# Trunk kernel: the two heads of a pair take turns in stick-breaking attention, and the sums for the seven products are spaced wider, their second parts on Pool

## The chip, the cores and the metric

One Trainium2 chip, one core. The metric is the device time of one launch in microseconds (us). A core has five engines that run beside each other, each through its own instructions in order: TensorE (PE, matmuls and transposes), VectorE (DVE), ScalarE (ACT), GpSimd (POOL) and SyncE (SP, which issues the DMAs). They wait for each other through semaphores.

## The reference

A decoder trunk of two layers on 1024 tokens of width 1024, all in float32. Cut to what matters:

```python
for l in range(DEPTH):                                   # 2
    h = rmsnorm(x, norm1[l])
    proj = h @ w_in[l]
    qa, ka, va, qb, kb, vb, gate_pre = jnp.split(proj, splits, axis=-1)
    o_a = dilated_mixture(qa, ka, va)                    # 3 groups of 4 heads of 64
    o_b = stick_breaking_attention(qb, kb, vb)           # 4 heads of 64
    gates = sigmoid(gate_pre + b_gate[l])
    x = x + (g_a * (o_a @ w_br[l, :256]) + g_b * (o_b @ w_br[l, 256:])) @ w_o[l]
    h2 = rmsnorm(x, norm2[l])
    a, v = split(h2 @ w_up[l])
    x = x + (gelu(causal_conv(a)) * v) @ w_down[l]
return rmsnorm(x, norm_f)

# stick_breaking_attention, one head:
z = q @ k.T * scale
log_stay = where(key < query, log_sigmoid(-z), 0)
later = reverse_cumsum(log_stay) - log_stay
o = where(key < query, exp(log_sigmoid(z) + later), 0) @ v
```

## The kernel before

**Numbers in two parts.** A float32 product is done as three matmuls: each operand is split into a first part `hi` (a ScalarE copy, line 123) and a second part `lo = src - hi` (a VectorE subtraction, line 124). `split` does both; it is used for weights (`w_hi`, `w_lo`), for transposed probabilities (`sbh`, `sbl` in the stick stage, `p0h`, `p0l` in the near stage) and for the sums below (`t_hi`, `t_lo`).

**Two streams on TensorE.** In the mixer of a layer, `attend` walks a list of attention items, and between an item's small steps it draws steps of the dense products from `Dense` (`dense.advance(rate)`; the rate for stick items is 0.68 of a dense step per small step). A dense step is six matmuls of a projection. The order of TensorE's instructions is the order in which they are written out. On the other engines the order is made by a planner when the program is built: it takes instructions in order of rank as they become ready by its own times, and what stands in `tc.high_priority(offset=AHEAD)` ranks 200 places earlier.

**Stick items.** There are sixteen in a layer: two pairs `pr`, two heads `s` of a pair, four blocks `qp` of 256 queries. `stick_item(pr, s, qp)` gives two score steps and qp + 1 pairs of a `turn` and an `apply`. A score step (`score(a)`, a block of 128 queries against L = 128 (2 qp + a + 1) keys) makes `z` on TensorE, masks its last 128 columns on VectorE (line 610), takes two sigmoids on ScalarE (`beta`, line 611, and `stay`, line 612), and then on VectorE a running product of `stay` from the right (the scan, line 614) and `beta * stay` (line 615). `turn` transposes blocks of `beta` on TensorE (line 625) and splits them; `apply` multiplies them with the values (line 636), and the last one of an item adds the halves up (`fold`). The score steps of the *next* item are written in between the steps of the present one. In the kernel before, one head of a pair goes through qp = 0, 1, 2, 3, and then the other.

After the sixteen stick items come four near items (`N00` to `N11`: scores `z`, `p`, the exponential of `p`, transposes `t`, products `o` on line 700) and sixteen far items.

**Sums of h.** Later dense units are computed in blocks, with seven products in place of eight. Their right-hand sides are sums of quarters of `h`, made once in a layer by `block_sums` in four series of four pieces (128 x 512 each). Series 3 and 1 need three Pool operations a piece (lines 871 to 873, `h_sum`); series 2 and 4 go on from them with two VectorE operations a piece (lines 882 and 883). Then each piece is split by `in_two`. The list that `series` makes has one entry for each call of `dense.aside()`, which goes with every `dense.advance`: piece i begins at entry i * gap and is split `lag` entries later. Series 3 may begin once item `B17`, the last stick item, is done, and series 1 once `N01`'s scores are. The first unit that uses the sums (`pair_v`, seven products, tiles `i_a`, `i_c`) comes after `N11`'s scores; its first Pool operation is line 936, `u`.

Of the kernel before, what the change touches and what calls it, by code (L numbers as in the profile page):

```python
# [11 lines left out]
ALU = mybir.AluOpType  # L12
# [28 lines left out]
RATE = (0.68, 0.85, 0.72, 0.62)  # L41
# [5 lines left out]
def f32(ap):  # L47
    return ap.bitcast(F32)
# [3 lines left out]
def trunk_kernel(ctx, tc, x, norm1, w_in, b_gate, w_br, w_o, norm2, w_up, conv_w, conv_b, w_down, norm_f, out, depth=None, probe=None):  # L52
    nc = tc.nc
    act, dve, pe, pool = nc.scalar, nc.vector, nc.tensor, nc.gpsimd
# [55 lines left out]
    def bank(tag, name):  # L110
        return ps.tile([P, 512], F32, tag=tag, name=name)
# [4 lines left out]
    def big(name, dtype=F32):  # L116
        return sb.tile([P, 2, T], dtype, tag="e8", bufs=6, name=name)

    def quarter(name, dtype=F32, c=HF):
        return sb.tile([P, 2048 // c, c], dtype, tag="xa", bufs=4, name=name)  # L120

    def split(hi, lo, src):
        act.copy(hi, src)  # L123
        dve.tensor_tensor(lo, src, f32(hi), ALU.subtract)  # L124
# [292 lines left out]
    S, B = {}, {}  # L417
# [152 lines left out]
    def scores(o, qt, ql, k):  # L570
        pe.matmul(o, qt, k, start=True, stop=False, skip_group_check=True)
        pe.matmul(o, ql, k, start=False, stop=True, skip_group_check=True)
# [17 lines left out]
    def stick_item(pr, s, qp):  # L590
        if "ob" not in R:
            R["ob"] = big("ob")
        q, k, vt, ob = R["qb", pr], R["kb", pr], R["vb"], R["ob"]
        hd = 2 * pr + s
        rows, st, shared = {}, {}, {}

        def score(a):
            i = 2 * qp + a
            L = P * (i + 1)
            bt = rows[a] = sb.tile([P, T], F32, tag="p4", bufs=4, name="beta")  # L600
            if a == 0:
                st[0] = big("stay")
            sv = st[0][:, a, :]
            for c0 in range(0, L, 512):
                w = min(512, L - c0)
                z = bank("s", "z")
                scores(z[:, :w], *(t[:, s, i * P : i * P + P] for t in q), k[:, s, c0 : c0 + w])
                with tc.high_priority(offset=AHEAD):
                    if c0 + w == L:
                        dve.tensor_tensor(z[:, w - P : w], z[:, w - P : w], mask_b, ALU.add)  # L610
                    act.activation(bt[:, c0 : c0 + w], z[:, :w], AF.Sigmoid)
                    act.activation(sv[:, c0 : c0 + w], z[:, :w], AF.Sigmoid, scale=-1.0)  # L612
            rev = sv[:, 0:L][:, ::-1]
            dve.tensor_tensor_scan(rev, rev, zero[:, 0:1].to_broadcast([P, L]), 1.0, ALU.mult, ALU.add)  # L614
            dve.tensor_tensor(bt[:, 0 : L - 1], bt[:, 0 : L - 1], sv[:, 1:L], ALU.mult)

        def blocks(kb):

            return [(j, a) for j in range(2) for a in range(2) if kb + j <= 2 * qp + a]

        def turn(kb):
            tp = bank("t", "sb_t")
            todo = blocks(kb)
            for c, (j, a) in enumerate(todo):
                pe.transpose(tp[:, c * P : c * P + P], rows[a][:, (kb + j) * P : (kb + j + 1) * P], ident)
            shared[kb] = parts(tp, len(todo) * P, "sb")

        def apply(kb):
            last = kb == 2 * qp
            if kb == 0:  # L630
                shared["o"] = bank("o", "sb_o")[:, :256]
            o = shared["o"]
            for j in range(2):
                c = P if last and j else 0
                for p in (0, 1):
                    pe.matmul(
                        o[:, c:256],
                        vt[(kb + j) // 4][:, (kb + j) % 4, hd, :],
                        shared[kb][p][:, 256 * j : 256 * j + 256 - c],
                        start=(kb == 0 and j == 0 and p == 0),  # L640
                        stop=(last and j == 1 and p == 1),
                        skip_group_check=True,
                    )
            if last:
                fold(ob[64 * s : 64 * s + 64, pr, qp * 256 : (qp + 1) * 256], o)
                if (pr, s, qp) == (1, 1, 3):
                    nc.sync.dma_start(obd, ob)

        sc = [lambda: score(0), lambda: score(1)]
        return sc, [(lambda kb=kb: turn(kb), lambda kb=kb: apply(kb)) for kb in range(0, 2 * qp + 2, 2)]  # L650
# [209 lines left out]
    def block_sums():  # L860


        keep = {}

        def first(t, a, b, i):
            if i == 0:
                if "r" not in keep:
                    keep["r"] = quarter("h_sum")
                new_s(t)
            r, (ah, al), (bh, bl) = keep["r"][:, i, :], a()[i], b()[i]  # L870
            pool.tensor_tensor(r, f32(al), f32(bl), ALU.subtract)
            pool.tensor_tensor(r, r, f32(ah), ALU.add)
            pool.tensor_tensor(r, r, f32(bh), ALU.subtract)

        def further(t, a, i):
            if t == 4:

                S[4] = half(0, 0)
            elif i == 0:
                new_s(t)  # L880
            r, (ah, al) = keep["r"][:, i, :], a()[i]
            dve.tensor_tensor(r, f32(ah), r, ALU.subtract)
            dve.tensor_tensor(r, r, f32(al), ALU.add)

        def in_two(t, i):
            split(*S[t][i], keep["r"][:, i, :])

        b11, b12, b21, b22 = (lambda n=n, k=k: half(n, k) for k in range(2) for n in (1, 0))
        todo = []

        def series(after, t, f, lag, gap):

            at = {}
            for i in range(4):
                at.setdefault(i * gap, []).append(lambda i=i: f(i))
                at.setdefault(i * gap + lag, []).append(lambda i=i: in_two(t, i))
            for k in range(3 * gap + lag + 1):
                todo.append((after, lambda fs=at.get(k, ()): [g() for g in fs]))

        series({"B17"}, 3, lambda i: first(3, b22, b12, i), 4, 3)  # L900
        series({"N01s"}, 1, lambda i: first(1, b12, b11, i), 4, 3)
        series({"N11s"}, 2, lambda i: further(2, b22, i), 1, 1)
        series({"plain"}, 4, lambda i: further(4, b21, i), 1, 1)
        return todo
# [180 lines left out]
    def mixer(l, pending):  # L1085
# [31 lines left out]
        items = []  # L1117
        for pr in range(2):
            for i in range(8):
                needs = ["b1"] if pr else []  # L1120
                items.append((f"B{pr}{i}", needs, [], RATE[0], lambda pr=pr, i=i: stick_item(pr, i // 4, i % 4)))
        for pr in range(2):
            for s in range(2):
                items.append((f"N{pr}{s}", [f"0{pr}"], ["v0"], RATE[1], lambda pr=pr, s=s: near_item(pr, s)))
# [590 lines left out]
    def first():  # L1715
        gb = sb.tile([P, T], F32, tag="ot", name="gb")
        warm = sb.tile([P, 8], F32, tag="ss", bufs=2, name="warm")
        act.activation(warm[:, 0:1], eps, AF.Sqrt)
        wp = bank("t", "warm")
        for _ in range(WARM):  # L1720
            pe.matmul(wp[:, 0:P], ident, ident, start=True, stop=True)
        for n in range(2):
            new_h(n)
            for c in range(4):
                t0 = n * HF + c * P
                xr = sb.tile([P, T], F32, tag="p4", bufs=4, name="xr")
                nc.sync.dma_start(xr, xin[t0 : t0 + P, :])
                if n == 0 and c == 0:
                    nc.sync.dma_start(gb, norm1[0].partition_broadcast(P))
                sq = sb.tile([P, T], F32, tag="ql", bufs=2, name="xsq")  # L1730
                ss = sb.tile([P, 8], F32, tag="ss", bufs=2, name="ss")
                act.activation(sq, xr, AF.Square, accum_out=ss[:, 0:1])
                act.activation(ss[:, 1:2], ss[:, 0:1], AF.Sqrt, bias=eps[:, 0:1], scale=1.0 / D)
                dve.reciprocal(ss[:, 2:3], ss[:, 1:2])
                for e0 in (0, 4):
                    hd = slice(e0 * P, (e0 + 4) * P)
                    dve.scalar_tensor_tensor(xr[:, hd], xr[:, hd], ss[:, 2:3], gb[:, hd], ALU.mult, ALU.mult)
                    tp = bank("s", "x_t")
                    for e in range(4):
                        pe.transpose(tp[:, e * P : (e + 1) * P], xr[:, (e0 + e) * P : (e0 + e + 1) * P], ident)  # L1740
                    tv = tp.rearrange("p (e t) -> p e t", e=4)
                    hi, lo = (h[:, e0 : e0 + 4, c * P : (c + 1) * P] for h in H[n])
                    split(hi, lo, tv)
                yield
# [46 lines left out]
```

## Time and profile before

| | |
|---|---|
| median of 3 runs | 2751.21 us (2749.49 to 2751.34) |
| the profiled execution | 2748.3 us, of it 2746.1 us from the first to the last instruction |
| granted TensorE clock, mean | 0.992 |
| busy: TensorE / VectorE / ScalarE / Pool | 2669.7 / 1989.7 / 1351.9 / 687.1 us |
| stick items, layer 0 / layer 1 | about 70 to 244 us / 1429 to 1605 us |
| near items, layer 0 / layer 1 | to about 330 us / 1690 us |

In the profile's rows the engine that is busy for nearly all of a stretch is the one that bounds it, and a row of the waits names, for an engine's pause, the instruction that waited and the one that it waited for, then the total in us, how often, and the longest. Window rows give a stretch, its length, and then the busy time of each engine in it; groups of instructions give the count, the busy time and the mean of one in ns; a tile's rows give shortest, median and longest in ns. The granted clock is a share of full speed.

### The profile page before, as it was taken

To read this page: it belongs to the slowest core of one execution; us is meant where nothing else is said; L and a number is where in the kernel's file an instruction comes from. 1 tells how busy PE (TensorE), PEld (TensorE's weight loads), DVE (VectorE), ACT (ScalarE), POOL (GpSimd) and SP (SyncE) were. 2 spreads that over 40 slices of the span, in tenths; PEclk is the share of its full clock that TensorE was granted. 3 is DMA by queue.
4 is the path that set the end of the run, shared out by engine and by line. 5 is a ranking of instruction groups with operands and counts; after the bars stand their busy time and mean duration, and the time that the engine had idled before them with its cause. 6 is when DMAs were issued, how large, how long until landed. Compare 5 with 4: busy or idle time off the path is not lost.

```text
span 2746.1 us, 36499 instructions
## 1 busy us (share of the span) xinstructions
PE 2669.7 (97%) x13066; PEld 2235.0 (81%) x13066; DVE 1989.7 (72%) x2952; ACT 1351.9 (49%) x2494; POOL 687.1 (25%) x485
## 2 busy tenths in 40 slices
PE   8999999989999999999999999999799999999999
PEld 8878888868878888878888788888688788887888
DVE  5877656555779888887657775565658788988865
ACT  5655545465445555422335555455535455554225
POOL 1005011222134433331120051112312443443200
PEclk9999999999999999999999999999899999999999
DMA  5012268664334444688401122785732444446963
GB/s 151 27 44 81 63 188 247 212 205 134 89 115 162 146 154 139 223 319 299 170 31 35 44 81 88 201 252 189 235 94 77 142 141 158 166 141 238 346 235 123
DMA packets 362305, 424.77 MB, mean 155 GB/s; under 512 B 25244, under 2 KB 289804, under 8 KB 360588
## 3 DMA queue, kind: packets, MB, share of 16 engines
q1 hardware_dynamic: 362124, 422.44, 46.9%
q8 instruction: 103, 1.69, 0.3%
q14 instruction: 78, 0.64, 0.1%
HBM read 282.78 MB, written 139.59 MB: 154 GB/s over the span
## 4 chain that ended last, share of the span: by engine, by line
PE 47%; DVE 5%; DMA 1%; issue 1%; ACT 1%; POOL 1%; DVEq 0%; SPq 0%; ACTq 0%; POOLq 0%
PE d_ps L1539 4%; PE d_ps L1541 4%; PE d_ps L1540 4%; PE u_a L854 3%; PE u_a L856 3%; PE u_a L855 3%; PE u_c L856 1%; PE u_c L854 1%; PE u_c L855 1%; PE i_a L854 1%; PE i_a L855 1%; PE i_a L856 1%; PE o_ps L149 1%; PE o_ps L151 1%; PE o_ps L150 1%
## 5 line engine op out<-in xcount | busy, mean ns | idle before, releaser
L123 ACT CAST w_hi<-up_a 128x512 fp32r<-128x512 f32 x240 | 149.5, 623 | 193.9 <-PE u_a L855 42.2
L124 DVE TENSOR_TENSOR w_lo<-up_a,w_hi 128x512 fp32r<-128x512 f32 x240 | 223.6, 938 | 20.4 <-ACT w_hi L123 20.4
L1547 DVE TENSOR_TENSOR x<-x,d_ps 128x512 f32<-128x512 f32 (+1 forms) x228 | 152.3, 672 | 78.0 <-PE d_ps L1541 77.3
L1285 POOL TENSOR_TENSOR cv<-cv 128x512 f32<-128x512 f32 x88 | 132.6, 1518 | 276.8 <-DVE g L124 144.7
L124 DVE TENSOR_TENSOR g<-cv,g 128x512 fp32r<-128x512 f32 x154 | 167.6, 1089 | 8.7 <-ACT g L123 6.2
L124 DVE TENSOR_TENSOR w_lo<-w_raw,w_hi 128x512 fp32r<-128x512 f32 x152 | 116.7, 773 | 66.9 <-ACT w_hi L123 63.4
L123 ACT CAST w_hi<-w_raw 128x512 fp32r<-128x512 f32 x152 | 93.9, 620 | 120.0 <-PE o_ps L150 64.4
L124 DVE TENSOR_TENSOR w_lo<-in_a,w_hi 128x512 fp32r<-128x512 f32 x120 | 90.9, 757 | 85.2 <-ACT w_hi L123 85.0
L123 ACT CAST w_hi<-in_a 128x512 fp32r<-128x512 f32 x120 | 74.5, 621 | 133.0 <-PE i_c L855 52.3
L1539 PE MATMUL d_ps<-gd_in,w_hi 128*128 128x512 f32 (+1 forms) x340 | 130.7, 384 | 6.1 <-ACT g L123 5.8
L1541 PE MATMUL d_ps<-gd_in,w_lo 128*128 128x512 f32 (+1 forms) x340 | 130.5, 384 | 0.0
L1540 PE MATMUL d_ps<-gd_in,w_hi 128*128 128x512 f32 (+1 forms) x340 | 130.3, 383 | 0.0
L856 PE MATMUL u_a<-hh,w_lo 128*128 128x512 f32 x320 | 124.7, 390 | 4.2 <-DVE w_lo L124 4.2
L854 PE MATMUL u_a<-t_hi,w_hi 128*128 128x512 f32 x320 | 124.7, 390 | 0.7 <-ACT u L1420 0.7
L854 PE MATMUL u_a<-hh,w_hi 128*128 128x512 f32 x320 | 124.6, 390 | 0.6 <-DVE u L1437 0.6
L856 PE MATMUL u_a<-t_hi,w_lo 128*128 128x512 f32 x320 | 124.5, 389 | 0.0
L855 PE MATMUL u_a<-hl,w_hi 128*128 128x512 f32 x320 | 124.5, 389 | 0.0
L855 PE MATMUL u_a<-t_lo,w_hi 128*128 128x512 f32 x320 | 124.5, 389 | 0.0
L614 DVE TENSOR_TENSOR_SCAN stay<-stay,zero 128x128 f32<-128x128 f32 (+3 forms) x64 | 86.8, 1357 | 38.7 <-ACT stay L612 38.6
L1539 PE MATMUL d_ps<-gd_in,wd 128*128 128x512 f32 (+1 forms) x292 | 113.9, 390 | 0.0
L1541 PE MATMUL d_ps<-gd_in,wd 128*128 128x512 f32 (+1 forms) x292 | 112.8, 386 | 0.0
L1540 PE MATMUL d_ps<-gd_in,wd 128*128 128x512 f32 (+1 forms) x292 | 112.8, 386 | 0.0
(397 smaller groups left out, 8593.7 us busy)
## 6 DMA issues: line engine op xcount, KB each, us to landing
gd<-g SPq DMA_DIRECT2D x154, 512.0 KB, 3.3
gd_in<-gd SPq DMA_DIRECT2D x154, 512.0 KB, 6.2
up_a<-in_w_up_dram SPq DMA_DIRECT2D x80, 512.0 KB, 5.4
t_kq<-tk SPq DMA_DIRECT2D x32, 768.0 KB, 6.3
wd_raw<-in_w_down_dram SPq DMA_DIRECT2D x22, 1024.0 KB, 9.5
w_raw<-in_w_in_dram SPq DMA_DIRECT2D x80, 256.0 KB, 3.3
in_a<-in_w_in_dram SPq DMA_DIRECT2D x40, 512.0 KB, 5.8
gin<-gs SPq DMA_DIRECT2D x32, 512.0 KB, 4.4
```

Source lines behind the costliest of these rows:

```text
L123: act.copy(hi, src)
L124: dve.tensor_tensor(lo, src, f32(hi), ALU.subtract)
L149: pe.matmul(o, lh, rh, start=(first and i == 0), stop=False, skip_group_check=share)
L614: dve.tensor_tensor_scan(rev, rev, zero[:, 0:1].to_broadcast([P, L]), 1.0, ALU.mult, ALU.add)
L854: pe.matmul(o, w[0][:, c], rh, start=(first and i == 0), stop=False, skip_group_check=True)
L855: pe.matmul(o, w[0][:, c], rl, start=False, stop=False, skip_group_check=True)
L856: pe.matmul(o, w[1][:, c], rh, start=False, stop=(last and i == 3), skip_group_check=True)
L1285: return lambda: pool.tensor_tensor(dst, a, b, ALU.subtract)
L1539: pe.matmul(o[:, sub], wh[:, c], gh[:, sub], start=(i == 0 and k in (0, 4, 5)), stop=False, skip_group_check=True)
L1540: pe.matmul(o[:, sub], wh[:, c], gl[:, sub], start=False, stop=False, skip_group_check=True)
L1541: pe.matmul(o[:, sub], wl[:, c], gh[:, sub], start=False, stop=(i == m - 1), skip_group_check=True)
L1547: dve.tensor_tensor(x, x, o[:, sub], ALU.add)
```

## The change

The two heads of a pair take turns: the items of a pair now run as (s, qp) = (0,0), (1,0), (0,1), (1,1), (0,2), (1,2), (0,3), (1,3). In `block_sums`, the pieces of series 3 and 1 begin five entries apart instead of three, and their second parts are subtracted on Pool instead of VectorE; the ScalarE copy is the same, and so are series 2 and 4.

```diff
         def in_two(t, i):
-            split(*S[t][i], keep["r"][:, i, :])
+            if t in (1, 3):
+                hi, lo = S[t][i]
+                act.copy(hi, keep["r"][:, i, :])
+                pool.tensor_tensor(lo, keep["r"][:, i, :], f32(hi), ALU.subtract)
+            else:
+                split(*S[t][i], keep["r"][:, i, :])
...
-        series({"B17"}, 3, lambda i: first(3, b22, b12, i), 4, 3)
-        series({"N01s"}, 1, lambda i: first(1, b12, b11, i), 4, 3)
+        series({"B17"}, 3, lambda i: first(3, b22, b12, i), 4, 5)
+        series({"N01s"}, 1, lambda i: first(1, b12, b11, i), 4, 5)
         series({"N11s"}, 2, lambda i: further(2, b22, i), 1, 1)
         series({"plain"}, 4, lambda i: further(4, b21, i), 1, 1)
...
         for pr in range(2):
             for i in range(8):
                 needs = ["b1"] if pr else []
-                items.append((f"B{pr}{i}", needs, [], RATE[0], lambda pr=pr, i=i: stick_item(pr, i // 4, i % 4)))
+                items.append((f"B{pr}{i}", needs, [], RATE[0], lambda pr=pr, i=i: stick_item(pr, i % 2, i // 2)))
```

## The prediction

> **What bounds the kernel now.** The page comes first, then the waits of TensorE, since only what ends one of its pauses can move the end.
>
> ```profile
> span 2746.1 us, 36499 instructions
> PE 2669.7 (97%) x13066; PEld 2235.0 (81%) x13066; DVE 1989.7 (72%) x2952; ACT 1351.9 (49%) x2494; POOL 687.1 (25%) x485
> PE sb_t L625 <- DVE beta L615: 12.5, 10, 2.4
> PE o L700 <- DVE p0l L124: 4.5, 2, 2.2
> PE o L700 <- ACT p0h L123: 0.5, 2, 0.3
> PE z L571 <- ACT stay L612: 1.2, 1, 1.2
> ```
>
> TensorE is busy 97% of the span and the change gives it the same matmuls, so all that can be won is its idle time, 2746.1 - 2669.7 = 76 us, and slow clock behind a pause. The last four lines (total, times, longest) are the only pauses in the two stretches that the diff touches: stick-breaking transposes waiting for VectorE's `beta`, and near-attention products waiting for `p0l`. Together 18.7 us, over two layers.
>
> Where do the first fall? The window view, cut at the first transpose of an item (layer 0: the last item of pair 0, then pair 1), gives per row the length and the busy time of PE, PEld, DVE, ACT, POOL, then the granted clock.
>
> ```profile
> 138.62:154.12 15.50, 14.04 (x79) 11.77 (x78) 10.16 (x20) 6.83 (x16) 0.00 (x0) 1.00 0.24 75
> 154.12:160.19 6.07, 6.07 (x32) 5.10 (x31) 4.47 (x7) 3.24 (x7) 0.00 (x0) 1.00 0.24 70
> 160.19:169.09 8.90, 8.90 (x49) 7.41 (x47) 7.54 (x11) 5.97 (x14) 0.00 (x0) 1.00 0.01 2
> 169.09:181.23 12.14, 10.86 (x61) 9.03 (x59) 9.89 (x14) 7.26 (x15) 0.00 (x0) 1.00 0.15 44
> 181.23:199.22 17.99, 15.55 (x79) 13.06 (x79) 11.94 (x21) 9.38 (x20) 0.00 (x0) 0.91 0.10 30
> 199.22:205.30 6.08, 6.08 (x32) 5.09 (x31) 4.53 (x8) 3.59 (x9) 0.00 (x0) 1.00 0.11 43
> 205.30:214.04 8.74, 8.74 (x48) 7.45 (x47) 7.65 (x11) 5.58 (x13) 0.00 (x0) 1.00 0.29 90
> 214.04:225.29 11.25, 11.14 (x62) 9.35 (x61) 8.75 (x11) 6.85 (x14) 1.90 (x2) 1.00 0.07 25
> ```
>
> The rows show one head climbing through its four query blocks (qp 0 to 3: about 6, 9, 11 and 15 us), and then the other. Length minus PE time is the pause at the start of a row: 1.46 at 138.62 (qp 3), 0, 0, 1.28 at 169.09 (qp 2), 2.44 at 181.23 (qp 3), 0, 0, 0.11. So it is the larger blocks that wait, at the top of a climb. Each row holds the scores of the *next* item beside the transposes of its own; VectorE is busy 74, 85 and 91% of PE's time over rows two to four, so its queue fills as the head climbs and empties in the long row.
>
> The clock costs more on top:
>
> ```profile
> 184.00:187.20 3.20, 3.20 (x9) 2.66 (x10) 2.43 (x5) 1.09 (x4) 0.00 (x0) 0.50 0.00 0
> 265.70:269.10 3.40, 3.40 (x10) 2.71 (x11) 1.57 (x3) 0.00 (x0) 3.40 (x4) 0.50 0.28 82
> 269.20:272.60 3.40, 3.40 (x21) 2.87 (x20) 1.37 (x2) 3.34 (x6) 3.14 (x3) 1.00 0.00 0
> 1543.60:1549.00 5.40, 4.64 (x17) 3.93 (x18) 4.53 (x9) 1.93 (x5) 0.00 (x0) 0.70 0.04 10
> 1605.00:1648.00 43.00, 40.51 (x216) 33.78 (x215) 35.24 (x58) 25.39 (x56) 27.71 (x21) 1.00 0.29 88
> ```
>
> After the pause of 2.44 us the clock is 0.50 for about 3.4 us; the same after layer 0's `p0l` pause (third row: 21 matmuls in the next 3.40 us against 10), and 0.70 on average behind layer 1's long stick pause. Half of 3.4 us is lost each time, 1.7. Layer 1's `p0l` pause costs no clock (last row, 1.00), nor does the 1.46 above. The Trainium skill, "TensorE: Matmul & The Clock Gate", Part 1, says that the array falls to half clock after an idle window of about 3.4 us; the pauses here are shorter and three of four lost it, so the trace decides. By that page no clock would come back and the sum below would be 5.1 us smaller.
>
> **Part 1: heads take turns.** An item does exactly what it did; only the order in a pair changes, from 0,1,2,3,0,1,2,3 to 0,0,1,1,2,2,3,3. The last item of a pair stays the last, so the sum of dense steps drawn before it, the units that wait for its scores and the store of `ob` keep their place to within two steps; the zero fill that waits for the third item comes some four steps earlier, on Pool, idle there. These cost nothing.
>
> What moves is VectorE's load per row. For the step into the qp 3 block the prices are:
>
> ```profile
> L614 DVE TENSOR_TENSOR_SCAN stay<-stay,zero 128x1024 f32<-128x1024 f32 x4 | 9.2, 2292 | 4.6 <-ACT stay L612 4.6
> L614 DVE TENSOR_TENSOR_SCAN stay<-stay,zero 128x896 f32<-128x896 f32 x4 | 8.1, 2025 | 3.4 <-ACT stay L612 3.4
> L614 DVE TENSOR_TENSOR_SCAN stay<-stay,zero 128x768 f32<-128x768 f32 x4 | 7.0, 1757 | 3.0 <-ACT stay L612 3.0
> L614 DVE TENSOR_TENSOR_SCAN stay<-stay,zero 128x640 f32<-128x640 f32 x4 | 6.0, 1492 | 1.3 <-ACT stay L612 1.3
> L615 DVE TENSOR_TENSOR beta<-beta,stay 128x1023 f32<-128x1023 f32 x4 | 4.9, 1217 | 0.0
> L615 DVE TENSOR_TENSOR beta<-beta,stay 128x895 f32<-128x895 f32 x4 | 4.3, 1084 | 0.1
> L615 DVE TENSOR_TENSOR beta<-beta,stay 128x767 f32<-128x767 f32 x4 | 3.8, 948 | 0.0
> L615 DVE TENSOR_TENSOR beta<-beta,stay 128x639 f32<-128x639 f32 x4 | 3.3, 820 | 0.1
> ```
>
> Scans and products of a qp 3 block are 2.29 + 2.03 + 1.22 + 1.08 = 6.6 us, of a qp 2 block 1.76 + 1.49 + 0.95 + 0.82 = 5.0. Before, every qp 2 row (10.9 us of PE) carries the 6.6; now one of two carries 5.0 and the other comes after that lighter row. A qp 3 row (14 us) carries 6.6 once, where it carried a small block before: 3 us of work more, but in the row with most room (10.16 of 14.04 busy). The equal steps are the new thing, and each is easier than the climb that it replaces: the same row, a shorter chain to the transposes. Into qp 0 and 1 the rows at 160.19 and 205.30 start without a pause even as climbs.
>
> So the climbs fall from twelve to six in a layer, and each stands behind a level step. Bounds for the 12.5 us: nothing saved (if the queue just fills elsewhere), or all of it. Half by count is 6.3 left; I take 5 left, since the worst (169.09, then 181.23) are two climbs in a row with a backlog handed on, which the new order doesn't have. Saved: 7.5, and both clock losses behind the 2.4 us pauses, 3.4. The 1.2 of `z` behind `stay` I leave as it is (0 to 1.2).
>
> **Part 2: sums of h.** The eight second parts of series 3 and 1 leave VectorE for Pool in each layer; the ScalarE copies stay. The near pause in layer 0, in VectorE's order of time, with the matmul that feeds `p` and ScalarE's wait:
>
> ```profile
> 253.15 4.21 DVE L124 TENSOR_TENSOR t_lo<-h_sum,t_hi 128x512 fp32r<-128x512 f32 x3
> 258.99 1.77 DVE L124 TENSOR_TENSOR t_lo<-h_sum,t_hi 128x512 fp32r<-128x512 f32 x1
> 255.86 0.28 PE L572 MATMUL z<-kt,ql 128*128 128x256 f32 x1
> 261.28 0.40 DVE L679 CUSTOM_DVE_ANT_0 p<-z,bias 128x256 f32<-128x256 f32 x1
> 261.73 0.51 ACT L680 ACTIVATE p<-p,st 128x256 f32<-128x256 f32 x1 [2.82 <-DVE st L679]
> 263.23 1.74 DVE L124 TENSOR_TENSOR w_lo<-w_raw,w_hi 128x512 fp32r<-128x512 f32 x1
> 264.89 0.68 DVE L124 TENSOR_TENSOR p0l<-t,p0h 128x512 fp32r<-128x512 f32 x1
> ```
>
> `z` is ready at 256.1, `p` starts 5.1 us later, because four `t_lo` (4.21 + 1.77 = 6.0 us) stand in the queue; the exponentials start late, then `p0h`, then `p0l`, and PE's product waits. Taking 6.0 us out ahead of a delay of 5.1 removes it. What is late next is the contended `w_lo`, 1.74, which then runs earlier. Bounds: 0 to all of 4.5 + 0.5 and the one clock loss, 6.7; I take 6.0.
>
> The other side is Pool, in order:
>
> ```profile
> L872 POOL TENSOR_TENSOR h_sum<-h_sum,hh x8: 1267/1295/1742, 241.6 to 269.8; 128x512 f32<-128x512 f32 x8
> L124 DVE TENSOR_TENSOR t_lo<-h_sum,t_hi x8: 681/743/1781, 253.2 to 277.6; 128x512 fp32r<-128x512 f32 x8
> ACT t_hi L123 <- POOL h_sum L873: 2.3, 2, 1.3
> 303.35 1.28 POOL L936 TENSOR_TENSOR u<-in_a 128x512 f32<-128x512 f32 x1 [30.94 <-DVE w_lo L124]
> ```
>
> Eight more operations of 1.27 to 1.74 are 10 to 14 us; the list whose last L872 sum starts at 269.8 ends some 10 to 14 us later, near 285, and Pool's next work starts at 303.35. So the Pool time is hidden; without that cover it would be 10 us late for the first pair's weights. Pool begins as soon as a buffer is free and runs on without rest, so the wider spacing (5 for 3) changes rank in the queues, not a rate: nothing. Against the move: VectorE's two-input operations take 0.68 alone and 1.78 while Pool runs (second row). The Trainium skill, "GPSIMD Engine Reference", Engine selection, puts such two-input work on VectorE, Pool being about twice as slow; 1.30 against 0.68 agrees. By that rule alone the eight would cost 5 us more than they free, if Pool's time counted.
>
> Sum: 7.5 + 3.4 + 6.0 = 16.9, so the profiled 2748.3 us becomes 2731. Against the median of 2751.2, which lies 2.9 higher, the same step gives **2734**.
>
> **The rivals.**
> *Only the near part pays.* VectorE's work is unchanged in sum, and the chain from scores to `beta` (over 6 us for qp 3) may set the pauses whatever the order. Against it: the same step into qp 2 paused 1.28 at 169.09 and 0.11 at 214.04, so the load beside it decides. 2751.2 - 6.0 = 2745.
> *Only the order pays.* Pool stays busy past 270 and stretches `w_lo`; the `p0l` pause stays. 2751.2 - 10.9 = 2740.
> *Nothing moves beyond a shift of pauses:* 2751. Each pause would have to find a new place.
> *Slower: Pool holds ScalarE.* In the near stage ScalarE's copy of each sum waits in order for Pool, whose list is now a third longer and itself waits for ScalarE; exponentials and `p0h` queue behind that copy. A pause so made is priced like the present one, 2.25 + 1.7 = 3.95 us. The rest of the change gives 10.9 + 6.7 = 17.6, so from the fifth pause in two layers on it is slower; with eight (every other of 16 sums) 2751.2 - 17.6 + 31.6 = 2765. For it: `t_hi` already waited 2.3 us for Pool in layer 0 (third row above); against it: ScalarE is busy only 25.4 of 43 us there (1605 row).
>
> **How the numbers follow.** Forecast 0.52, near part alone 0.12, order alone 0.14, nothing 0.09, slower 0.13. About 0.2%, 5.5 us, is what a measurement of this kernel can tell from no change: the first three are faster by more, 0.78; same 0.09; slower 0.13. The range goes down to everything saved (12.5 + 1.2 + 3.4 + 6.7 = 23.8: 2727, and a little for the scatter of runs) and up past "near part alone": 2726 to 2748; outside lie the slower case and half of "nothing".
>
> **What would show it.** Right: waits of `sb_t` for `beta` near 5 us with none over 2, clock 1.00 through both stick stages; `p0l` gone from TensorE's waits; the eight `t_lo` on Pool, ending before 300. Wrong: `beta` still near 12; `p0l`, `p0h` or `t` waits grown with ScalarE waiting for `h_sum`; or a first `i_c` product waiting for `t_lo`.

## The result and the profile after

The changed kernel takes 2764.62 us (median of 6 runs, 2760.47 to 2771.43); the kernel before, on the same chip at the same time, 2750.32 us. The ratio is 1.0054, 95% interval 1.0041 to 1.0067: slower by half a per cent, where the prediction said faster, outside its range, and near the time of its slower rival (2765). The six runs lie in two groups, three from 2760.47 to 2761.70 us and three from 2767.54 to 2771.43; the profiled execution is the lowest of the upper group, and what its rows show below is shown for that execution alone.

The first two lines of the page of the changed kernel, and then those of its waits of TensorE that lie in the two stretches of the change (total us, times, longest):

```profile
span 2765.8 us, 36519 instructions
PE 2673.6 (97%) x13066; PEld 2239.0 (81%) x13066; DVE 1995.0 (72%) x2936; ACT 1351.3 (49%) x2494; POOL 707.2 (26%) x501
PE o L700 <- ACT p0h L123: 14.0, 2, 13.6
PE sb_t L625 <- DVE beta L615: 11.4, 12, 1.8
PE o L700 <- DVE p0l L124: 9.8, 5, 5.6
PE g_ps L151 <- DVE w_lo L124: 1.8, 2, 0.9
```

The span grew by 2765.8 - 2746.1 = 19.7 us: 3.9 in TensorE's busy time (two of the kernels below with the same order and the same waits near line 700, e1 and e4, differ by 3.2 in it) and 15.8 in its idle time. The near products on line 700 waited 5.0 us before (`p0l` 4.5, `p0h` 0.5) and wait 23.8 now, 18.8 more. The stick stage gained a little: `beta` 12.5 to 11.4, the 1.2 of `z` behind `stay` is gone, and 1.8 of `g_ps` behind `w_lo` is new, so 0.5 less in sum. Two single pauses carry the loss of this execution, one in each layer: 13.6 us for `p0h` in layer 0, and 5.6 us for `p0l` in layer 1.

**Layer 0.** VectorE, and Pool in the stretch where VectorE's long operation ends (start, duration, engine, line, operation, tile and what it reads). The last row of the first block is of the kernel before, the subtraction at the same place, right behind the `p0l` of 384 columns:

```profile
256.08 16.31 DVE L124 TENSOR_TENSOR w_lo<-w_raw,w_hi 128x512 fp32r<-128x512 f32 x1
272.31 0.41 DVE L679 CUSTOM_DVE_ANT_0 p<-z,bias 128x256 f32<-128x256 f32 x1
257.81 1.25 DVE L124 TENSOR_TENSOR w_lo<-w_raw,w_hi 128x512 fp32r<-128x512 f32 x1
```

```profile
269.32 1.30 POOL L873 TENSOR_TENSOR h_sum<-h_sum,hh 128x512 f32<-128x512 f32 x1
270.54 1.30 POOL L872 TENSOR_TENSOR h_sum<-h_sum,hh 128x512 f32<-128x512 f32 x1
271.92 1.60 POOL L873 TENSOR_TENSOR h_sum<-h_sum,hh 128x512 f32<-128x512 f32 x1
```

The subtraction that took 1.25 us at this place in the kernel before took 16.31. Pool's operations there follow each other some 1.22 us apart at a duration of 1.30, so there is no time between them, until one ends at 270.54 + 1.30 = 271.84 and the next starts at 271.92. Then VectorE's operation ends, at 272.39. All that stood behind it was late: `p`, ScalarE's exponential, `p0h`, the product.

**Layer 1** has no such operation. There the rows are of ScalarE's wait (first line, total, times, longest), VectorE, Pool and ScalarE:

```profile
ACT t_hi L888 <- POOL h_sum L873: 6.1, 4, 2.2
1647.67 3.41 DVE L882 TENSOR_TENSOR h_sum<-hh,h_sum 128x512 f32<-128x512 f32 x2 [5.05 <-POOL t_lo L889]
1651.00 1.75 DVE L883 TENSOR_TENSOR h_sum<-h_sum,hl 128x512 f32<-128x512 f32 x1
1652.78 0.56 DVE L124 TENSOR_TENSOR p0l<-t,p0h 128x384 fp32r<-128x384 f32 x1
1646.35 5.85 POOL L889 TENSOR_TENSOR t_lo<-h_sum,t_hi 128x512 fp32r<-128x512 f32 x4
1646.95 0.47 ACT L123 CAST p0h<-t 128x384 fp32r<-128x384 f32 x1
```

`p0h` was ready at 1647.42, but `p0l` started at 1652.78: in VectorE's queue three operations of the sums of series 2 stood ahead of it. They overwrite `h_sum`, which Pool's `t_lo` still had to read, so VectorE was idle 5.05 us waiting for Pool; and then each took 1.7 us instead of 0.68, beside Pool's other `t_lo`. Before, VectorE made `t_lo` itself and this wait could not arise.

**The clock and the stick stage.** Window rows as in the prediction: the long row of the stick stage in layer 0; the first near work after each long pause; and four steps of layer 0's turn-taking order, cut at the same kind of place: the two items of qp 0 that begin pair 0, then in pair 1 the second item of qp 0 and the first of qp 1.

```profile
183.00:199.00 16.00, 16.00 (x91) 13.71 (x90) 14.76 (x20) 12.42 (x27) 0.00 (x0) 1.00 0.11 34
275.00:281.40 6.40, 6.21 (x19) 5.04 (x20) 2.86 (x5) 3.00 (x6) 0.00 (x0) 0.50 0.72 194
1653.40:1657.00 3.60, 3.60 (x11) 2.99 (x11) 3.54 (x6) 0.27 (x1) 0.00 (x0) 0.50 0.24 72
72.20:76.90 4.70, 4.70 (x24) 3.72 (x24) 4.38 (x12) 2.61 (x7) 0.00 (x0) 1.00 0.00 0
76.90:81.90 5.00, 4.40 (x24) 3.47 (x23) 4.21 (x9) 3.32 (x7) 0.00 (x0) 1.00 0.18 52
161.42:165.80 4.38, 4.38 (x25) 3.73 (x23) 3.90 (x7) 3.64 (x8) 0.00 (x0) 1.00 0.00 0
165.80:176.13 10.33, 8.53 (x46) 7.03 (x45) 8.79 (x15) 5.22 (x11) 0.00 (x0) 1.00 0.19 53
```

The stick stage keeps full clock (1.00 over the stick stages of both layers), as predicted. The near stage loses (6.4 + 3.6) / 2 = 5.0 us of clock, about what the kernel before lost at the three places that the prediction listed.

Where Pool's list ends and what comes next on Pool, in layer 0:

```profile
284.29 6.40 POOL L889 TENSOR_TENSOR t_lo<-h_sum,t_hi 128x512 fp32r<-128x512 f32 x4 [10.77 <-ACT t_hi L888]
317.50 1.28 POOL L941 TENSOR_TENSOR u<-in_a 128x512 f32<-128x512 f32 x1 [26.80 <-DVE w_lo L124]
```

The list ends at 290.7 and Pool then rests 26.8 us. So the list is done well before Pool's next work, as the prediction had it (near 285), and the conclusion drawn from this, that Pool's time is hidden, is still wrong.

### The profile page after: what moved, and what is told of

Same layout as the page of the kernel before. It is cut to its first block, busy times and chain, and to the rows that moved or that the text cites. A ratio compares the mean times of both kernels' runs of the same rounds, so it can differ in the third digit from the quotient of the medians.

```text
span 2765.8 us, 36519 instructions
## 1 busy us (share of the span) xinstructions
PE 2673.6 (97%) x13066; PEld 2239.0 (81%) x13066; DVE 1995.0 (72%) x2936; ACT 1351.3 (49%) x2494; POOL 707.2 (26%) x501
## 4 chain that ended last, share of the span: by engine, by line
PE 82%; DVE 8%; issue 3%; POOL 3%; ACT 2%; DMA 2%; SPq 0%; DVEq 0%; ACTq 0%; POOLq 0%
PE u_a L856 5%; PE u_a L855 5%; PE u_a L854 5%; PE d_ps L1544 5%; PE d_ps L1546 5%; PE d_ps L1545 5%; PE u_c L855 3%; PE u_c L854 3%; PE u_c L856 3%; PE i_a L854 2%; PE i_a L855 2%; PE i_a L856 2%; PE o_ps L149 2%; PE o_ps L150 2%; PE o_ps L151 2%
## 5 line engine op out<-in xcount | busy, mean ns | idle before, releaser
L124 DVE TENSOR_TENSOR w_lo<-w_raw,w_hi 128x512 fp32r<-128x512 f32 x152 | 131.6, 869 | 74.9 <-ACT w_hi L123 71.3
```

## The experiments

**The parts alone, and the spacing.** Four kernels: the order alone; the sums alone; the whole change with the old spacing; and the whole change with the second parts back on VectorE, so that only order and spacing are left.

```diff
 e1_order (from the kernel before)
-  stick_item(pr, i // 4, i % 4)
+  stick_item(pr, i % 2, i // 2)
 e2_sums (from the changed kernel)
-  stick_item(pr, i % 2, i // 2)
+  stick_item(pr, i // 4, i % 4)
 e3_gap3 (from the changed kernel)
-  series({"B17"}, 3, ..., 4, 5);  series({"N01s"}, 1, ..., 4, 5)
+  series({"B17"}, 3, ..., 4, 3);  series({"N01s"}, 1, ..., 4, 3)
 e4_dve (from the changed kernel)
-  if t in (1, 3): act.copy(hi, ...); pool.tensor_tensor(lo, ...)
+  split(*S[t][i], keep["r"][:, i, :])
```

> The turn-taking alone, sums as before. Theory A (the loss comes from the second parts on Pool: its list in the near stage is longer and unbroken, and VectorE operations with two SBUF inputs wait behind it): the order saves the 1.1 us of transposes' waits that the changed profile shows less (11.4 against 12.5), the 1.2 us of z behind stay and the two clock losses of 1.7 us, so about 2745 to 2747, and the near stage's pauses are those of before (5.0 us). Theory B (the order costs, since it shifts the near items against the dense units): 2758 or more, with near pauses over 15 us.

> The sums alone (spacing 5, second parts on Pool), the heads one after the other as before. Theory A: the whole loss is here and the small gain of the order is not: 2764 to 2770, with single runs spread over some 10 us, and VectorE operations of more than 2 us in the near stage in some executions. Theory B: 2751 or less.

> The changed kernel with the spacing put back to 3, second parts still on Pool. Theory A: Pool begins as soon as a buffer is free and runs on, so the spacing does little: 2760 to 2770. Theory C (it is the wider spacing that puts sums and splits at a bad place in the queues): 2748 or less.

> The changed kernel with the second parts back on VectorE; spacing 5 and turn-taking stay. Theory A: the loss is gone: 2745 to 2750. Theory C: the loss stays, 2758 or more.

| | us, median | ratio to before | 95% interval |
|---|---|---|---|
| e1_order | 2743.35 | 0.9983 | 0.9974 to 0.9992 |
| e2_sums | 2758.40 | 1.0044 | 1.0027 to 1.0061 |
| e3_gap3 | 2758.71 | 1.0052 | 1.0033 to 1.0071 |
| e4_dve | 2744.15 | 0.9985 | 0.9977 to 0.9994 |

(before: 2748.25.) The waits of TensorE of the first, then of the second:

```profile
PE sb_t L625 <- DVE beta L615: 11.4, 12, 1.8
PE o L700 <- DVE p0l L124: 4.5, 2, 2.3
PE g_ps L151 <- DVE w_lo L124: 1.8, 2, 0.9
```

```profile
PE o L700 <- ACT p0h L123: 13.9, 2, 13.6
PE sb_t L625 <- DVE beta L615: 12.5, 10, 2.4
PE o L700 <- DVE p0l L124: 10.3, 5, 5.6
```

Order and sums do not touch each other's pauses. The order alone is faster, by about 5 us. With the second parts on VectorE the wider spacing changes nothing that the intervals can tell (e4 against e1), and with them on Pool the narrower one doesn't help (e3). So the whole loss is the second parts on Pool. In e2 it is smaller than expected (2764 to 2770), since only one of its six runs is that long. The long subtraction came again in e2, 16.32 us, in its longest run (2772.08), whose profile this is. The profile of e3 is of its shortest run (2755.48) and has none; both its layers have the 5.6 us pause instead. The long operation is thus not needed for the loss. It seems to add to it where it comes: e2's other five runs lie from 2756.64 to 2760.55 us, and the two groups of the changed kernel's runs would fit executions with it and without. But one run of each kernel was profiled, so this is not shown.

**Half of the second parts.** Only those of series 3 on Pool, or only those of series 1, the rest as in the changed kernel.

```diff
-            if t in (1, 3):
+            if t == 3:        # n1_third;  in n2_first:  if t == 1:
```

> Turn-taking and spacing 5; only series 3 has its second parts on Pool, series 1 on VectorE. Theory A1 (the loss is the four second parts of series 1: they keep Pool busy while VectorE does the sums of series 2, which stand in front of p0l): the pause of 5.6 us is gone and the first pause is 1.0 in place of 2.3, so 2737 to 2742, below the 2743 of the order alone. Rival A2 (any lengthening of Pool's list costs): 2750 or more, and VectorE operations of 16 us in some executions.

> Turn-taking and spacing 5; only series 1 has its second parts on Pool, series 3 on VectorE. Theory A1: the pause of 5.6 us of p0l stays in both layers and the first one is 2.3: 2753 to 2760. Rival A2: like the one before it, since the list is equally long.

n1_third: 2755.99 us against 2745.54, ratio 1.0033 (1.0022 to 1.0045). n2_first: 2751.47, ratio 1.0018 (1.0009 to 1.0027). The waits of n1_third, TensorE's and, in layer 0's near stage, ScalarE's; then TensorE's of n2_first:

```profile
PE o L700 <- ACT p0h L123: 4.9, 4, 1.4
PE o L700 <- DVE p0l L124: 3.8, 6, 1.0
ACT t_hi L123 <- POOL h_sum L873: 5.0, 2, 2.8
```

```profile
PE o L700 <- DVE p0l L124: 10.3, 6, 2.2
```

Theory A1 failed in both: n1 is far from 2737 to 2742, and in n2 the pause of 5.6 did not stay. The rival, that any lengthening of Pool's list costs, fits the times, though neither profile has a long operation. In n1 the pause of 5.6 is gone, as is VectorE's wait for Pool's `t_lo` of series 1. In its place come pauses for `p0h`: Pool's sums of series 1 are some 4 us later behind the four `t_lo` (the last starts at 273.1 us, in e4 at 268.9), and ScalarE, which copies each sum in order, now waits up to 2.8 us for them, with `p0h` queued behind. The expected gain of the four moved subtractions shows too: the first near pause of 2.25 fell to 1.04. In n2 the 2.25 stays, and a second pause of 2.2 follows in each layer, for `p0l`. VectorE's row of the sums in front of it, in layer 0:

```profile
273.92 3.47 DVE L882 TENSOR_TENSOR h_sum<-hh,h_sum 128x512 f32<-128x512 f32 x2
```

These operations take 1.7 us each beside Pool's `t_lo`, as in layer 1 of the changed kernel, and what stands behind them in VectorE's queue is late: the `p0l` of the pause starts at 283.43 us, in e1 at 279.94. But VectorE did not have to wait for Pool before them, and there is no pause of 5.6: in these captures that needs all eight second parts on Pool. Neither half pays.

The pauses give only a part of these two losses. From the first to the last start of line 700, n1 takes 84.2 and 84.1 us in the two layers and n2 85.7 and 85.5, where e4 takes 81.4 and 81.5. That is 5.4 and 8.3 us of the 12.4 and 12.6 by which their spans are longer than e4's, whose capture is of another chip; the rest lies in other stages, and no run shows why.

**Pool's run broken.** The changed kernel, with a copy of one column on Pool from each piece into the next, so that a piece cannot start before the last is done and Pool's operations no longer run into each other.

```diff
             pool.tensor_tensor(r, r, f32(bh), ALU.subtract)
+            if i < 3:
+                pool.tensor_copy(keep["r"][:, i + 1, 0:1], r[:, 0:1])
```

> The changed kernel with a one-column copy on Pool between the sums of one piece and of the next, so that every operation of a sum waits for the one just before it and Pool's run has a short break at each; the results do not change. Theory L (Pool's unbroken run shuts VectorE's operation with two SBUF inputs out until the first break): no VectorE operation over 2.3 us in the near stage and single runs within 5 us of each other, 2750 to 2758. Rival (the 16 us are something else, a transfer or a semaphore): 16 us again in some executions, single runs spread over 10 to 20 us.

2761.01 us (2757.47 to 2763.64), ratio 1.0051 (1.0039 to 1.0063).

```profile
PE o L700 <- DVE p0l L124: 16.0, 6, 5.6
```

In the attention stages no operation of VectorE is longer than 2.29 us, a scan of the stick stage: the long one is gone. The scatter is 6.2 us, where the changed kernel had 11.0 and e2 and e3 15 and 22. But the pauses of 5.6 are in both layers, and the time is above the 2750 to 2758 expected and that of the changed kernel within the intervals. So the long operation does not explain the loss by itself.

**Another order of the stick items,** sums as before: one head up, the other down.

```diff
-  stick_item(pr, i // 4, i % 4)
+  stick_item(pr, i // 4, min(i, 7 - i))      # and ob's store moved to the last item
```

> Sums as before; the blocks go 0, 1, 2, 3 with one head and 3, 2, 1, 0 with the other (and the store of ob follows the new last item), so that there are six climbs in a layer as in turn-taking, but no two small items of a pair one after the other. If the pauses of turn-taking come from two short items in a row (latency), transposes wait 6 us or less, and the time is 2738 to 2743. If they come from climbs of any kind, about 11 us and 2743 to 2746.

2760.58 us, ratio 1.0050 (1.0038 to 1.0062).

```profile
PE z L571 <- DVE st L679: 15.2, 2, 7.6
PE o L700 <- DVE p0l L124: 8.4, 2, 4.6
PE sb_t L625 <- DVE beta L615: 2.8, 6, 0.9
249.68 8.54 DVE L124 TENSOR_TENSOR w_lo<-w_raw,w_hi 128x512 fp32r<-128x512 f32 x1 [0.54 <-ACT w_hi L123]
255.20 2.47 POOL L873 TENSOR_TENSOR h_sum<-h_sum,hh 128x512 f32<-128x512 f32 x2
```

The stick stage is far better: 2.8 us in place of 12.5, so the order of the items does set those pauses. This order has six climbs in a layer like the turn-taking one, so it is not their number. That two short items in a row do it, as the expectation has it, fits; but here too two items of qp 0 meet, at the change of pairs, and the wait behind them is only 0.43. The gain is lost in the near stage. The buffer of the sums comes free earlier here, Pool starts at 223 (in the changed kernel at 237.4), and ScalarE waits 6.4 us in one piece for a sum (the longest pause for `z` is 7.6). So the time is 2760.58 where 2738 to 2746 was expected. And with no second part on Pool at all, VectorE has an operation of 8.54 us, in both layers. It ends at 258.22; Pool's list ends at 257.67.

**Is it Pool's unbroken run that holds VectorE?** Two kernels from n5_hill: one lengthens Pool's last run, one breaks it once.

```diff
 k2_hill_long
-            pool.tensor_tensor(r, f32(al), f32(bl), ALU.subtract)
+            for _ in range(5 if (t, i) == (1, 3) else 1):
+                pool.tensor_tensor(r, f32(al), f32(bl), ALU.subtract)
 k3_hill_onebreak
             pool.tensor_tensor(r, r, f32(bh), ALU.subtract)
+            if (t, i) == (1, 2):
+                pool.tensor_copy(keep["r"][:, i + 1, 0:1], r[:, 0:1])
```

> The hill order of n5_hill, with the first Pool operation of the last piece of series 1 issued five times instead of once (same result): Pool's last unbroken run gets four operations of about 1.25 us longer, 5 us, and nothing else is changed. Theory L (a VectorE subtraction that starts while Pool runs back to back is held until Pool's run ends): the w_lo of 8.54 us near 250 in layer 0 and near 1613 in layer 1 becomes about 13.5 us in both layers and ends within 0.3 us of Pool's last operation; the p0l pause behind it grows from 4.6 and 3.8 us to about 9, and the time goes from 2760.6 to about 2770. Rival (the long operation is of a fixed length, or has another cause than Pool's run): it stays at 8 to 9 us or disappears, and the time stays within 4 us of 2761.

> The hill order of n5_hill, with one copy of one column on Pool between the third and the last piece of series 1: Pool's last unbroken run is broken once, some 4 us before its end. Theory L (a VectorE subtraction is held until the first break in Pool's run): the longest VectorE subtraction in the near stage ends at that break, at most about 5 us long in place of 8.54, or there is none. Rival (any long run of sums does it, breaks or not): it stays at 8 to 9 us and ends with Pool's last operation. The time moves little either way, 2757 to 2762, since ScalarE is held by the same late sums.

k2: 2764.84 us, ratio 1.0056 (1.0033 to 1.0079). k3: 2756.16 us, ratio 1.0019 (1.0008 to 1.0030). VectorE and Pool of k2, then of k3:

```profile
251.01 8.53 DVE L124 TENSOR_TENSOR w_lo<-w_raw,w_hi 128x512 fp32r<-128x512 f32 x1 [0.55 <-ACT w_hi L123]
256.51 1.26 POOL L874 TENSOR_TENSOR h_sum<-h_sum,hh 128x512 f32<-128x512 f32 x1
257.73 2.93 POOL L872 TENSOR_TENSOR h_sum<-hl,hl 128x512 f32<-128x512 f32 x2
259.07 1.60 POOL L872 TENSOR_TENSOR h_sum<-hl,hl 128x512 f32<-128x512 f32 x1
```

```profile
250.74 2.37 DVE L124 TENSOR_TENSOR w_lo<-w_raw,w_hi 128x512 fp32r<-128x512 f32 x1 [0.55 <-ACT w_hi L123]
251.27 1.29 POOL L871 TENSOR_TENSOR h_sum<-hl,hl 128x512 f32<-128x512 f32 x1
252.64 1.62 POOL L872 TENSOR_TENSOR h_sum<-h_sum,hh 128x512 f32<-128x512 f32 x1
```

k2 came out as the rival said, 8.53 and not 13.5, and the rows say why: the repeated operations write the same piece, so each waits for the one before. The first of them ends at 257.73 + 1.26 = 258.99 and the second starts at 259.07; there the run has its first gap, and VectorE's operation ends at 259.54. The edit lengthened the list but not the run without a gap. k3 met the theory: its operations depend on each other, the first gap comes after the first of them (252.56 to 252.64), VectorE's operation ends at 253.11 after 2.37 us, and the long one is gone from both layers. The copy did more than its place suggests: all six operations of this last run now have gaps between them. It brought the ratio from 1.0050 to 1.0019, some 8.5 us (the two kernels ran on different chips, so their medians compare less directly); the two `p0l` pauses of n5, 4.6 + 3.8 us, are gone with it.

In all of these captures (one each in the changed kernel and e2, one in each layer of n5, k2 and k3) the held subtraction ends 0.55 us after the end of the Pool operation that has the first gap behind it: 272.39 after 271.84, 258.22 after 257.67, 259.54 after 258.99, 253.11 after 252.56. The gap is 0.08 us wide, or the end of the list. That Pool's run held VectorE in these captures is therefore shown; why other stretches without a gap let VectorE in (in k2 a `w_lo` that began at 246.75, in the same kind of run, took 1.62) is open.

**Tries at a better version.** f1_back puts series 1, 2 and 4 into the pieces of `h_sum` from the back, on e1_order; f2_back_only does it on the kernel before.

```diff
+        def place(t, i):
+            return i if t == 3 else 3 - i
...
-            r, (ah, al), (bh, bl) = keep["r"][:, i, :], a()[i], b()[i]
+            r, (ah, al), (bh, bl) = keep["r"][:, place(t, i), :], a()[i], b()[i]
...                                                      # the same in further and in_two
```

> Turn-taking, second parts on VectorE, spacing 3; series 1 (and 2 and 4, which go on from it) use the four places of the sum buffer from the back, so that Pool can begin series 1 only when VectorE has split the last piece of series 3; results unchanged. Theory N (the near pause of 2.3 us comes from the four t_lo, stretched to 1.8 us each by Pool running on): Pool rests for some 2 us, three t_lo take about 0.7 us, and the pause falls under 1 us with no clock loss behind it, so 2735 to 2740 against the 2743 of turn-taking alone. Rival (the pause comes from the contended w_lo and bias just ahead of p0l): still 2.3 us, 2742 to 2746.

> The kernel before with the sum buffer used from the back alone. Theory N: near pauses as in the one with turn-taking, transposes' waits as before (12.5 us), 2740 to 2745 against the 2746 to 2748 of before. Rival: no change.

f1: 2745.63 us, ratio 0.9982 (0.9974 to 0.9991); f2: 2749.44, ratio 1.0000 (0.9991 to 1.0010). Beside e1 and the kernel before nothing moved: Pool ran on without a rest, presumably because the planner took the piece whose place was free first, and the near pause of layer 0 stayed 2.26. They say nothing on their theory.

g1_gate makes Pool rest: on e1_order, each piece of series 1 first copies a column from the last `t_lo` of series 3. g2_hillgate does the same on n5_hill and holds series 3 back until the last stick item is folded.

```diff
+            if t == 1:
+                pool.tensor_copy(r[:, 0:1], f32(S[3][3][1])[:, 0:1])
+            else:                                            # g2_hillgate alone
+                pool.tensor_copy(r[:, 0:1], R["ob"][:, 1, 0:1])
```

> Turn-taking, second parts on VectorE; before each piece of series 1 Pool copies one column of the last t_lo of series 3 into the piece's place (then overwritten), so that series 1 can begin only when VectorE has split the last piece of series 3; results unchanged. Theory N (the near pause of 2.3 us comes from the four t_lo, stretched to 1.8 us while Pool runs on): three t_lo take some 0.7 us, the pause falls under 1 us without a clock loss: 2735 to 2741 where turn-taking alone has 2743 to 2746. Rival (the contended w_lo and bias just ahead of p0l): still 2.3 us, 2743 to 2747.

> The order 0, 1, 2, 3, 3, 2, 1, 0, and the sums of series 3 held, by a one-column copy from ob, until the last stick item is folded, those of series 1 as in the one before; results unchanged. If the loss of the hill order was Pool's early, unbroken run beside the last stick items (ScalarE held 6.4 us, a VectorE operation of 8.5 us), both are gone and the transposes' waits stay near 3 us: 2733 to 2741. Rival (the hill order itself delays the near items): pauses of z over 5 us stay, 2752 or more.

g1: 2747.70 us, ratio 0.9996 (0.9987 to 1.0005). g2: 2753.40, ratio 1.0016 (1.0007 to 1.0025). The waits of g1, TensorE's and, in layer 0's near stage, ScalarE's:

```profile
PE o L700 <- ACT p0h L123: 4.9, 4, 1.3
PE o L700 <- DVE p0l L124: 3.1, 6, 0.7
ACT t_hi L123 <- POOL h_sum L875: 7.3, 4, 3.9
```

With Pool at rest while VectorE makes `t_lo`, its four `t_lo` of series 3 took 3.10 + 0.69 us in layer 0 instead of the 4.21 + 1.77 of e1, and the first near pause fell from 2.26 to 0.74: it is Pool beside it that made VectorE late there. But the sums then came later, ScalarE waited 7.3 us for them instead of 2.3, and `p0h` pauses took back the gain and most of the order's as well. g2 is the same at a larger size: no `z` pause of 7.6, no long operation, but a `p0h` pause of 6.2 in each layer.

No version tried is faster than the order alone beyond the intervals. e1_order, with 0.9983 (0.9974 to 0.9992), beats both kernels, the one before by some 5 us; e4 and f1, with 0.9985 and 0.9982, have the same order and agree with it.

## Why the prediction was wrong

**Part 1, the order: right in direction, half in size.** Forecast 10.9 us, measured about 5 (e1). The clock part held: the 3.4 us lost to half clock behind the two pauses of 2.4 us are saved. The term that was mis-sized is "5 left" of the 12.5: 11.4 are left, twelve pauses with none over 1.8. The bound "nothing saved (if the queue just fills elsewhere)" was nearly the true one. What failed in the reasoning is "Into qp 0 and 1 the rows at 160.19 and 205.30 start without a pause even as climbs", and with it that each level step is easier than the climb that it replaces. The largest blocks went as predicted: the transposes of qp 3 wait 0.21 us at most. But the smaller ones wait now. In layer 0 the second item of qp 0 waits 0.60 us, the climbs to qp 1 0.94 and 1.80, the level step to the second qp 1 in pair 1 0.86, and one climb to qp 2 1.22. The prediction's rows left out the first climb of pair 0, where the kernel before already waits 0.94 us for its first block of qp 1 (0.51 in layer 1). That short items give VectorE too little time fits the rows above (VectorE is busy 4.38 of 4.70 us, 4.21 of 5.00 and 3.90 of 4.38), but is not shown: in the same 4.70 us the kernel before has VectorE busy 4.57. A new wait of 1.8, `g_ps` for `w_lo`, came on top, which I had listed nowhere, while the 1.2 of `z` went away.

**Part 2, the sums: wrong in sign; this is the failed step.** Forecast 6.0 us gained, measured about 10 lost alone (e2: 2758.40 against 2748.25), and some 19 against the same order with the second parts on VectorE (1.0054 of the changed kernel against e4's 0.9985). That four `t_lo` off VectorE help the first pause was right in kind (2.25 to 1.0 us in e3 and n1). What failed is "the Pool time is hidden". I looked for cover at the end of Pool's list: it ends before Pool's next work, by 26.8 us. But the list is read piece by piece while it runs, by engines that work in order. ScalarE copies each `h_sum`, with `p0h` behind the copy; VectorE overwrites each `h_sum` in series 2, with `p0l` behind that. When Pool's pieces come later, this reaches TensorE by one of the two: in n1 by ScalarE, in e3, n3 and layer 1 of the changed kernel mostly by VectorE, and in g1 by ScalarE without any second part moved. I asked which work *follows* the moved operations on Pool, and not who waits for those behind them in the list. The wait "VectorE's L882 for Pool's `t_lo`", 5.05 us idle, is a wait that the change adds, and I did not list it. What follows it in layer 1 is shown, `p0l` 5.36 us after `p0h` and a pause of 5.6.

I had also taken the contention at 1.78 against 0.68 us as the whole price of Pool beside VectorE. In the changed kernel it was once 16.31. The Trainium skill, "SBUF — State Buffer", Who interferes with whom, says that a VectorE operation with two inputs from that memory and a GpSimd operation that reads it contend for one shared path, which one of them holds alone for a whole instruction. The 1.7 us agrees with that: one Pool operation of 1.27 waited out in part, and then 0.68 of work. The 16.31 is longer than any one Pool operation: VectorE was passed over for thirteen of them that followed each other without a gap.

I had set the two-to-one price of Pool aside, 5 us more than the eight free, because Pool's time would not count. It counted, but as the waits of other engines, 10 to 19 us, and not as Pool's own time. The Trainium skill, "GPSIMD Engine Reference", Engine selection, advises against such elementwise work with two inputs on Pool, as about twice as slow, and pointed the right way here.

**Spacing: right.** 5 for 3 changed nothing that the intervals can tell (e4 against e1, and e3 against the changed kernel).

**The rivals.** The slower one, "Pool holds ScalarE" with 2765, gave the time by luck, and only part of the mechanism. It counted eight pauses of 3.95 us. There are two long ones, 13.6 and 5.6, and both come through VectorE; ScalarE's wait for `h_sum` is 6.1 us in layer 1 and 1.9 in layer 0, where it was 2.3. ScalarE as the holder is shown in n1 and g1, not in the changed kernel. "Only the order pays" (2740) named the right part that pays.

**How much is the long operation?** In the hill order, breaking up Pool's run took it away and some 8.5 us with it (n5 to k3, by the ratios). In the changed kernel the ratio did not move when it was broken up (n3: 1.0051 against 1.0054). But n3 adds six copies a layer and makes the pieces run one after the other, and this may cost by itself: its near products wait 19.5 us, those of e3's capture 14.6, and neither has a long operation. That share stays open, as does why layer 0 had it and layer 1 not.

## What to carry to other kernels

An engine that rests after its list need not have free time inside it: before moving work onto a slower engine, go through every piece that stands behind the moved one, name the in-order engine that reads or overwrites it, and price what is queued behind that read. Where a profile shows a VectorE operation held by a long run of two-input Pool operations, try gaps in that run: in n3, k2 and k3, operations that depended on the one before left them by themselves, two interleaved pieces did not. It paid in the hill order and not in the changed kernel. And when an order of work is changed, go through the short rows as carefully as the long ones, since pauses that go at the top of a climb can come back at its foot.

## What the runs showed of the hardware

- A VectorE subtraction with two inputs in on-chip memory, 0.68 us alone and up to 1.78 beside Pool, was held 16.31 us (changed kernel), 16.32 (e2) and about 8.5 (n5 and k2, both layers) while Pool's two-input operations ran 1.22 to 1.25 us apart without a gap. It ended 0.55 us after the end of the Pool operation that had the first gap, 0.08 us wide, or the end of the list behind it. Not every such run held VectorE.
- `p0l`, which reads its first operand from a matmul's result, took 0.56 us for 384 columns (changed kernel, at 255.56 us) and 0.68 for 512 (k2 and k3) with Pool busy beside it: it was late only by what stood in front of it.
- The clock fell to half after pauses of 2.40 and 2.44 us in the kernel before, and after one of its two pauses of 2.25. In n1 it was 0.78 over the 3.43 us behind pauses of only 1.09 and 1.35 us some 4 us apart, and the stick pauses of up to 1.80 us in the changed kernel cost none: the length of a pause alone does not decide it.
